# A channel-mixing stage in float32 halves: the third piece's u and gate as seven products of half size, interleaved with the other pieces' products

## The chip, the core and the metric

The kernel runs on one core of one Trainium2 chip. The metric is the time of one launch in microseconds (us), measured on the device; three runs of the kernel before gave 943.95, 944.12 and 947.55 us, so its median is 944.12 us.

## What is computed

Two residual layers over 1024 prompt tokens and 64 sample tokens (8 sequences of 8), width 1024. The first is gated linear attention, which the change leaves alone but for the form of its last result. The second is a chunked token-mixing MLP:

```python
def cmlp_mixer(h, w_in, ln_g, ln_b, w_spatial, b_spatial, w_out):
    u, v, gate = jnp.split(h @ w_in, 3, axis=-1)
    v = layernorm(v, ln_g, ln_b)
    ...
    mixed = jnp.einsum('gts,bnsgd->bntgd', ws, vg) + bs.T[:, :, None]
    z = u * mixed.reshape(bsz, t, CMLP_WIDTH) * jax.nn.silu(gate)
    return z @ w_out, v
```

`h` is the RMS-normalised input of the layer. All operands are float32.

## The kernel before, in words

The 1088 tokens are three pieces: 384, 384 and 320 (two chunks of 128 and the 64 sample rows). Activations lie with features on the partitions and tokens in the free dimension. A float32 operand is split into a rounded part and a rest (float32r, `split` L189, `parts_of` L943), and a product of two of them is three matmuls per 128 features: high by high, high by low, low by high.

The v columns of the MLP are made first, in blocks 16 to 19 (L996 to L1038). While that runs, `token_sums` (L912) loads the layer's input again and forms sums of features and of the first two pieces in `tsum`, for what follows.

Then a loop over m = 0 to 7 (L1106 on; a *step* below) makes 128 columns of u and the same 128 columns of gate, multiplies, and stores z. For pieces 0 and 1, the two column blocks (u, gate), the two halves of the features and the two pieces form a 2 by 2 by 2 product, which is made from seven block products in place of eight, each over 4 times 128 features (`product` L986: 12 matmuls of 128x384). The operands of the weights for it are four sums of quarters of the weight block (s1 to s4, `sums` L961, on POOL) and three plain quarters (1,1), (1,2), (2,2). Piece 2 has an odd width and takes the ordinary way: `u` (L1197, L1198) and `gate` (L1204, L1205) are two accumulations of 24 matmuls of 128x320 each, for which a fourth plain quarter (2,1) is needed.

The weight block of a step is a single buffer, `rawq` (L937, `Quarters` L949): 1 MB in four loads. It is loaded for one step ahead when the last plain quarter has been taken out of it. The split operands are in a ring of eight buffers (`wq`, L944). The PSUM banks used here are two each of `misc` (`pb`, `pe`), `mm` (`p1`, `u`, `gate`) and `o` (`mix`).

The normalised v comes back by DMA into `vm` (L1060, two buffers), is normalised by nine ScalarE instructions (`v_norm` L1069) and mixed over the positions of a chunk on TensorE (`mixed` L1084). A small result `v_out` (L1079) is made of it on POOL.

From L993 to the end of the loop, `in_order` (L48) ties each engine to the order in which the code is written: DVE, ACT, POOL, PE and the DMA queue of SP each run their instructions of this stage in exactly that order. After the loop, `out_proj` (L791) multiplies z by the last weights: piece 0 from an operand that is split during the last step, pieces 1 and 2 from z reloaded by DMA (L1236 on).

## Time and profile before

| | before |
|---|---|
| median of three runs | 944.12 us |
| the profiled execution | 945.69 us, of which the span from first to last instruction is 943.9 us |
| granted TensorE clock, mean | 0.995 |
| TensorE busy (matmul) | 909.9 us, 96% of the span |
| VectorE, ScalarE, GpSimd busy | 624.3, 447.0, 305.6 us |
| v blocks 16 to 19 | about 536 to 637 us |
| the loop over m | 637.0 to 832.5 us |
| output projection | from 832.5 us on |

PE is TensorE's matmul, PEld its weight load, DVE VectorE, ACT ScalarE, POOL GpSimd, SP the engine that issues the DMAs. L12 is line 12 of the kernel before. The busy time of the matmuls overlaps itself, since they are pipelined: what a matmul costs in a stream is the distance from its start to the next one's start. In the profile's shapes "128x384" is 128 partitions by 384 elements.

### The profile page before, as it was taken

Reading aid. Unit: us, or ns where it says so; the run is one execution under the profiler, and the core shown is the slowest. Engines: PE = TensorE matmul, PEld = TensorE weight load, DVE = VectorE, ACT = ScalarE, POOL = GpSimd, SP = SyncE. Lnnn points to the kernel's source line nnn. Section 1 sums busy time; section 2 is a strip of 40 time slices with the busy share of each in tenths; the row PEclk is TensorE's granted clock in tenths of the full one; section 3 lists DMA queues with packets and bytes.
Section 4 is the critical chain, followed back from the end, with each engine's and each line's share of the span. In section 5 each row is a group of like instructions: output and inputs, shape, how many; then the busy total and the mean of one; then the engine's idle time right before and its main releaser. Section 6 shows DMA issues by size and latency. Waiting matters only on the chain.

```text
span 943.9 us, 16451 instructions
## 1 busy us (share of the span) xinstructions
PE 909.9 (96%) x6149; PEld 884.2 (94%) x6149; DVE 624.3 (66%) x1239; ACT 447.0 (47%) x940; POOL 305.6 (32%) x315
## 2 busy tenths in 40 slices
PE   9989999999999999989999999999899999989995
PEld 8979989998999899978999999999899999989994
DVE  7888778677885877688552944455666666773246
ACT  7664544454462555464342733336444444454322
POOL 2023332333322331322143121144655555302123
PEclk9999999999999999999999999999999999999998
DMA  9302113311232112324574143523333333384233
GB/s 296 95 1 82 50 36 87 110 38 36 67 103 60 63 41 84 103 83 126 154 255 141 62 152 121 177 73 100 97 97 97 97 97 97 116 259 123 58 109 129
DMA packets 89644, 98.40 MB, mean 104 GB/s; under 512 B 9927, under 2 KB 82061, under 8 KB 89565
## 3 DMA queue, kind: packets, MB, share of 16 engines
q1 hardware_dynamic: 89564, 97.36, 33.6%
q8 instruction: 48, 0.79, 0.3%
q14 instruction: 32, 0.25, 0.1%
HBM read 70.92 MB, written 26.42 MB: 103 GB/s over the span
## 4 chain that ended last, share of the span: by engine, by line
PE 66%; DVE 15%; ACT 6%; issue 6%; DMA 5%; POOL 2%; SPq 1%; DVEq 0%; ACTq 0%; POOLq 0%
PE fm L132 26%; PE tm L146 15%; PE pb L990 4%; PE p L990 3%; PE pe L990 3%; PE u L990 2%; PE gate L990 2%; PE sc L508 2%; PE tms L162 1%; DVE wq L946 1%; PE pst L579 1%; PE mix L1088 1%; DMA xsum<-x_spill 1%; PE o L618 1%; DVE scT L521 1%
## 5 line engine op out<-in xcount | busy, mean ns | idle before, releaser
L146 PE MATMUL tm<-w,h 128*128 128x256 f32 (+1 forms) x1536 | 192.7, 283 | 1.6 <-ACT vt L1001 1.2
L132 PE MATMUL fm<-h,w 128*128 128x384 f32 (+1 forms) x1056 | 188.7, 333 | 0.1
L146 PEld LDWEIGHTS tm<-w,h 128*128 128x128 f32 x1536 | 185.4, 188 | 3.4 <-ACT vt L1001 1.6
L132 PEld LDWEIGHTS fm<-h,w 128*128 128x128 f32 x1056 | 174.4, 188 | 2.0 <-DVE h L196 0.7
L132 PE MATMUL fm<-og,w 128*128 128x384 f32 (+1 forms) x576 | 102.0, 332 | 0.4 <-DVE og L193 0.4
L132 PEld LDWEIGHTS fm<-og,w 128*128 128x128 f32 x576 | 95.1, 188 | 1.6 <-DVE og L193 0.6
L118 DVE TENSOR_TENSOR w<-wr,w 128x512 fp32r<-128x512 f32 (+1 forms) x96 | 71.3, 758 | 21.4 <-ACT w L117 20.6
L117 ACT ACTIVATE w<-wr 128x512 fp32r<-128x512 f32 (+1 forms) x96 | 58.6, 624 | 26.6 <-DMA wr<-w 14.5
L132 PE MATMUL fm<-zs,w 128*128 128x384 f32 (+1 forms) x384 | 64.0, 326 | 1.4 <-DVE x L838 1.4
L816 POOL TENSOR_TENSOR acc<-acc,sq 128x384 f32<-128x384 f32 (+1 forms) x30 | 30.9, 1034 | 105.6 <-ACT sq L811 105.1
L132 PEld LDWEIGHTS fm<-zs,w 128*128 128x128 f32 x384 | 62.3, 188 | 2.6 <-DVE x L838 2.0
L838 DVE TENSOR_TENSOR x<-fm,res 128x384 f32<-128x384 f32 (+1 forms) x40 | 21.0, 527 | 54.5 <-PE fm L132 54.5
L811 ACT ACTIVATE sq<-x 128x384 f32<-128x384 f32 (+1 forms) x42 | 21.0, 503 | 62.2 <-DVE x L838 59.4
L1008 DVE BATCH_NORM_STATS2 st<-vt 128x6 f32<-128x256 f32 (+1 forms) x36 | 15.2, 421 | 42.4 <-ACT vt L1001 42.2
L463 POOL TENSOR_TENSOR xe<-xe,k 128x384 f32<-128x384 f32 (+2 forms) x24 | 28.5, 1187 | 45.2 <-ACT xe L462 42.0
L649 POOL TENSOR_TENSOR on<-on,g 128x384 f32<-128x384 f32 (+1 forms) x24 | 23.8, 1013 | 57.0 <-DVE on L648 34.6
L439 POOL TENSOR_TENSOR kd<-kd,k 128x384 f32<-128x384 f32 (+1 forms) x12 | 12.0, 1004 | 85.8 <-ACT kd L438 85.8
L990 PE MATMUL pb<-tsum,wq 128*128 128x384 f32 x192 | 37.2, 341 | 2.5 <-DVE wq L946 1.4
L990 PEld LDWEIGHTS pb<-tsum,wq 128*128 128x128 f32 x192 | 33.7, 188 | 3.7 <-DVE wq L946 1.8
L990 PE MATMUL p<-h,wq 128*128 128x384 f32 x192 | 36.4, 337 | 0.0
L990 PE MATMUL pe<-tsum,wq 128*128 128x384 f32 x192 | 36.2, 336 | 0.0
L132 PE MATMUL fm<-tsum,w 128*128 128x384 f32 x192 | 34.3, 338 | 1.6 <-DVE z L1199 1.6
(271 smaller groups left out, 1855.2 us busy)
## 6 DMA issues: line engine op xcount, KB each, us to landing
wr<-w SPq DMA_DIRECT2D x92, 256.0 KB, 3.1
rawq<-w SPq DMA_DIRECT2D x32, 256.0 KB, 3.5
s<-s SPq DMA_DIRECT2D x16, 256.0 KB, 5.9
state_s<-ns SPq DMA_DIRECT2D x32, 128.0 KB, 2.5
v_spill<-vt SPq DMA_DIRECT2D x32, 128.0 KB, 1.8
vm<-v_spill SPq DMA_DIRECT2D x8, 512.0 KB, 4.3
xsum<-x_spill SPq DMA_DIRECT2D x8, 384.0 KB, 3.6
z_spill<-zt SPq DMA_DIRECT2D x16, 192.0 KB, 1.9
```

Source lines behind the costliest of these rows:

```text
L117: A.activation(w[:, 0], raw, AF.Copy)
L118: V.tensor_tensor(w[:, 1], raw, w[:, 0].bitcast(F32), ALU.subtract)
L132: PE.matmul(acc, lhs, rhs, start=(k == 0), stop=(k == 23))
L146: PE.matmul(acc, lhs, rhs, start=(k == 0), stop=(k == 23))
L463: G.tensor_tensor(xe, xe, kt_[:, :nl], ALU.mult)
L508: PE.matmul(bank[:, c, 0:192], xe[:, c * P:(c + 1) * P], xl[:, c * 192:(c + 1) * 192], start=True, stop=True)
L649: G.tensor_tensor(o, o, gate[h][:, j, t0:t0 + n], ALU.mult)
L811: A.activation(sq, raw[p][:, m, :], AF.Square)
L816: (V if gain is not None and p == 2 or m == KT - 1 else G).tensor_tensor(total, acc[p], sq, ALU.add)
L838: V.tensor_tensor(raw[p][:, m, :], pa, r, ALU.add)
L990: PE.matmul(acc, lhs, rhs, start=start and k + i == 0, stop=k + i == 5, skip_group_check=not start)
L1008: V.bn_stats(stats[i][:, blk - 16, :], t)
```

## The change

Piece 2 is also made as a 2 by 2 by 2 product. Its 320 columns are re-ordered into two halves of 160, each of one chunk (128) and half of the sample rows (32), and take the place of the two pieces. Per step this is seven products of 12 matmuls of 128x160 in place of the 48 matmuls of 128x320, with the same seven weight operands as the products of pieces 0 and 1. In the code each of the seven products of 384 columns (`pb`, `pe`, `pa`) is followed by one of 160 (`qb`, `qe`, `qa`; the first two in a pair of banks called `two`).

What goes with it:

- The operands of the new sums (`half_load`, `half_sums`, `half_parts`) are made during blocks 18 and 19 and mostly written over parts of `h1` that have been used up; block 19 is computed in the order 6, 7, 8, 3, 4, 5, 0, 1, 2 so that they are. Only `sum4` is new memory. The column scales `rs[2]` are re-ordered in place.
- The quarter (2,1) is no longer split. `vm` has one buffer instead of two, and `v_norm` of a step runs in that step.
- The copies, adds and multiplications of piece 2 follow those of pieces 0 and 1. The mixed values of all pieces go into one tile `zt`, and the SiLU and the last product are one instruction each for all of them: `zt` and `sg` are 2 by 544.
- From step 1 on, the four sums of the next weight block stand early in the step on POOL, ahead of `v_out`. The load of the block after it is issued at the end of the step, behind four stores of z.
- At the end, piece 1's operand for the output projection takes its last block from `zt` directly.

The step's instructions on PE. In both lists one step starts at the first `pb`; `p_...` is the accumulator `pa`, `q_...` is `qa`, `two` is `qb` or `qe`, `xN` counts matmuls, or, for `mix`, products of two matmuls each. Before, step 1:

```order
L990 MATMUL pb<-tsum_6126,wq 128x384 x12
L990 MATMUL pe<-tsum_6127,wq 128x384 x12
L990 MATMUL pb<-tsum_6125,wq 128x384 x12
L990 MATMUL p_7693<-h_0_5912,wq 128x384 x12
L1088 MATMUL mix<-ws,vm 128x128 x6
L990 MATMUL pb<-h_1_6014,wq 128x384 x12
L990 MATMUL pe<-tsum_6128,wq 128x384 x12
L990 MATMUL p_7693<-h_0_5912,wq 128x384 x12
L1088 MATMUL mix<-ws,vm 128x128 x2
L1091 MATMUL mix<-wss,vm 128x64
L990 MATMUL u<-h_2_6079,wq 128x320 x24
L990 MATMUL gate<-h_2_6079,wq 128x320 x24
```

After, a step up to its fifth pair of products:

```order
L1047 MATMUL pb<-tsum_6142,wq 128x384 x12
L1047 MATMUL two<-h_1_6014,wq 128x160 x12
L1047 MATMUL pe<-tsum_6143,wq 128x384 x12
L1047 MATMUL two<-h_1_6014,wq 128x160 x12
L1047 MATMUL pb<-tsum_6141,wq 128x384 x12
L1047 MATMUL two<-h_2_6079,wq 128x160 x12
L1047 MATMUL p_8157<-h_0_5912,wq 128x384 x12
L1047 MATMUL q_8158<-h_2_6079,wq 128x160 x12
L1158 MATMUL mix<-ws,vm 128x128 x6
L1047 MATMUL pb<-h_1_6014,wq 128x384 x12
L1047 MATMUL two<-h_2_6079,wq 128x160 x12
L1158 MATMUL mix<-ws,vm 128x128 x2
```

The two long groups `u` and `gate` are gone; a group of twelve 128x160 stands behind each of the seven groups of 128x384.

On POOL, one turn from the multiplication of `zt` on. `qsum` and `qs` are the sums s1 to s4 of a weight block, `bc` is `v_out`, `p_...` and `q_...` are u and gate values. Before:

```order
L1162 TENSOR_TENSOR zt<-zt,p_7627 128x384
L958 TENSOR_TENSOR qsum<-rawq 128x512
L958 TENSOR_TENSOR qsum<-qsum,rawq 128x512
L1175 TENSOR_TENSOR sg<-sg,rs_80 128x384
L958 TENSOR_TENSOR qsum<-rawq 128x512
L958 TENSOR_TENSOR qs_7783<-rawq,qsum 128x512
L1064 MEMSET vm 64x128
L1221 TENSOR_TENSOR sg_7854<-sg_7854,rs_81 128x320
L1080 TENSOR_TENSOR bc<-vm,bc 64x128
L1081 TENSOR_TENSOR bc<-bc 64x128
L1152 TENSOR_TENSOR p_7866<-p_7866,p_7867 128x384
```

After, from the last multiplication of `sg` of the step before on:

```order
L1277 TENSOR_TENSOR sg<-sg,rs_80 128x384
L1014 TENSOR_TENSOR qsum<-rawq 128x512
L1014 TENSOR_TENSOR qsum<-qsum,rawq 128x512
L1014 TENSOR_TENSOR qsum<-rawq 128x512
L1014 TENSOR_TENSOR qs_8370<-rawq,qsum 128x512
L1149 TENSOR_TENSOR bc<-vm,bc 64x128
L1150 TENSOR_TENSOR bc<-bc 64x128
L1227 TENSOR_TENSOR p_8333<-p_8333,p_8334 128x384
L1228 TENSOR_TENSOR sg<-sg,p_8334 128x384
L1229 TENSOR_TENSOR q_8335<-q_8335,q_8336 128x160
L1230 TENSOR_TENSOR sg<-sg,q_8336 128x160
L1231 TENSOR_TENSOR sg<-sg,rs_80 128x384
```

The sums moved from behind the multiplication of `zt`, late in a step, to the front of the next one, ahead of `bc` and the five additions and multiplications of that step.

On SP's DMA queue, one step from the stores of z on. Before:

```order
L1186 DMA z_spill<-zt 128x384 x2
L1065 DMA vm<-v_spill 128x8x128
L1066 DMA vm<-v_spill 64x128
L1076 DMA bc<-lnbc 64x256
L940 DMA rawq<-w 128x512 x4
L1223 DMA z_spill<-z_7531 128x320
```

After:

```order
L1286 DMA z_spill<-zt 128x384 x2
L1288 DMA z_spill<-zt 128x2x128
L1288 DMA z_spill<-zt 128x2x32
L996 DMA rawq<-w 128x512 x4
L1145 DMA bc<-lnbc 64x256
L1151 DMA v_out<-bc 64x128
```

The load of the weight block now follows four stores of z.

The core of the diff. Of the loop only the lines after are shown; those before are the listing above, L1100 to L1228.

```diff
+NH = 160
...
     def side_by_side(act, name, into):
         hs = into.tile([P, KT, 2, NS], F32R, tag="hs", name=name)
         for part in range(2):
-            G.tensor_copy(hs[:, :, part, :], act[:, part, :, 256:320].bitcast(F32))
+            for lo, hi, at in ((0, NS, 256),) if into is gc else ((0, 32, P), (32, NS, 160 + P)):
+                G.tensor_copy(hs[:, :, part, lo:hi], act[:, part, :, at:at + hi - lo].bitcast(F32))
...
+    def halves(t, natural):
+
+        if natural:
+            return (t[:, lo:hi].rearrange("p (h t) -> p h t", h=2) for lo, hi in ((0, 256), (256, 320)))
+        t = t.rearrange("p (h t) -> p h t", h=2)
+        return t[:, :, :P], t[:, :, P:]
...
+            gain = ng[:, 1, kt:kt + 1]
+            if p < 2:
+                split(h1[p], kt, raw[:, kt, :], gain)
+                continue
+
+            hi, lo = (halves(h1[p][:, i, kt, :], 0) for i in range(2))
+            for dh, dl, src in zip(hi, lo, halves(raw[:, kt, :], 1)):
+                A.activation(dh, src, AF.Copy, scale=gain)
+                V.scalar_tensor_tensor(dl, src, gain, dh.bitcast(F32), ALU.mult, ALU.subtract)
...
+    sum4 = mp.tile([P, 2, 4, NH], F32R, tag="sum4", name="sum4")
+    even = lambda t, lo: [t[:, i].rearrange("p (k e) t -> p k e t", e=2)[:, :, 0, lo:lo + NH] for i in range(2)]
+    tsum2 = [even(h1[2], NH), even(h1[1], 0), even(h1[1], NH), [sum4[:, 0], sum4[:, 1]]]
+    xh = {}
+
+    def half_load(k):
+
+        if k == 0:
+            x = vp.tile([P, 2, 2, NPMAX], F32, tag="xsum", name="xhalf")
+            for i in range(2):
+                xh[i] = [x[:, i, e, :2 * NH].rearrange("p (h t) -> p h t", h=2) for e in range(2)]
+        elif k > 1:
+            xh[k] = [tmp(("ld", "sq")[k - 2], (3, 2)[k - 2], 2 * NH, "xhalf").rearrange("p (h t) -> p h t", h=2)
+                     for _ in range(2)]
+        for e in range(2):
+            row = a["x1_spill"][:, 2 * k + e, SEQ - 256:]
+            for lo, hi, at in ((0, P, 0), (P, NH, 256)):
+                n = 2 * (hi - lo)
+                SP.dma_start(xh[k][e][:, :, lo:hi], row[:, at:at + n].rearrange("p (h t) -> p h t", h=2))
+
+    def half_sums(k):
+        for e in range(2):
+            A.activation(xh[k][e], xh[k][e], AF.Copy, scale=ng[:, 1, 2 * k + e:2 * k + e + 1])
+        b11, b12, b21, b22 = (xh[k][e][:, h, :] for e in range(2) for h in range(2))
+        G.tensor_tensor(b11, b12, b11, ALU.subtract)
+        G.tensor_tensor(b12, b22, b12, ALU.subtract)
+        G.tensor_tensor(b22, b22, b11, ALU.subtract)
+        G.tensor_tensor(b21, b21, b22, ALU.subtract)
+
+    def half_parts(i):
+
+        hi, lo = tsum2[i]
+        for k in range(4):
+            src = xh[k][i in (1, 3)][:, (0, 1, 1, 0)[i], :]
+            A.activation(hi[:, k], src, AF.Copy)
+            V.tensor_tensor(lo[:, k], src, hi[:, k].bitcast(F32), ALU.subtract)
...
-        for i in range(9):
+        for j, i in enumerate((6, 7, 8, 3, 4, 5, 0, 1, 2) if blk == 19 else range(9)):
             t = vp.tile([P, 256], F32, tag="vt", bufs=4, name="vt")
             if i < 8:
-                A.activation(t, tm_block(ws_[blk], h1[i // 3], (i % 3) * P), AF.Copy)
...
+            if blk == 18 and j in (0, 1):
+                half_load(2 + j)
+            if (blk, j) == (18, 2):
+
+                t = tmp("hn", 2, 2 * NH, "rsh")
+                for dst, src in zip(halves(t, 0), halves(rs[2], 1)):
+                    G.tensor_copy(dst, src)
+                G.tensor_copy(rs[2], t)
+            if (blk, j) == (18, 5):
                 nxt = Quarters(20)
             if blk == 19:
+                if j < 2:
+                    half_load(j)
+                if j in (0, 1):
+                    half_sums(2 + j)
+                if j in (2, 3):
+                    half_sums(j - 2)
+                if j in (4, 5, 6, 7):
+                    half_parts((3, 0, 1, 2)[j - 4])
+                if j in (1, 2, 3):
+                    nxt.sums(("s1", "s2", "s3")[j - 1])
+                if j in (3, 4, 5, 6):
+                    if j == 5:
+                        nxt.sums("s4")
+                    if j == 6:
+                        nxt.plain((1, 1))
+                    else:
+                        nxt.parts(("s1", "s2", "s3")[j - 3])
...
-        t = up.tile([P, 9, P], F32, tag="vm", bufs=2, name="vm")
+        t = up.tile([P, 9, P], F32, tag="vm", name="vm")
...
     zs = [None] * 3
+    N, M = NPMAX, NPMAX + NH
+    tq = [[(t[:, 0, k, :], t[:, 1, k, :]) for k in range(4)] for t in tsum]
+    tq2 = [[(hi[:, k], lo[:, k]) for k in range(4)] for hi, lo in tsum2]
+    b11, b21, b22 = quarter(0, 0), quarter(0, 1), quarter(1, 1)
+    half = lambda e, lo: [(x[..., lo:lo + NH], y[..., lo:lo + NH]) for x, y in quarter(2, e)]
+    c11, c21, c22 = half(0, 0), half(1, 0), half(1, NH)
+    rsh = rs[2].rearrange("p (h t) -> p h t", h=2)
     vm = v_load(0)
+    cur, nxt = nxt, None
     for m in range(KT):
+        w, g, more = cur.w, m // 2, m + 1 < KT
+        first = m == 0
+        bias = up.tile([P, P], F32, tag="bias", name="bias")
+        zt = up.tile([P, 2, M], F32, tag="zt", name="zt")
+        sg = up.tile([P, 2, M], F32, tag="sg", name="sg")
         bc = v_out_load(m)
         pb, pe = ps("misc", "pb")[:, :N], ps("misc", "pe")[:, :N]
+        two = pp.tile([P, 2, 512], F32, tag="sc4", name="two")
+        qb, qe = two[:, 0, :NH], two[:, 1, :NH]
         p6, p1 = tmp("sq", 2, N, "p6"), tmp("sq", 2, N, "p1")
+        q6, q1 = tmp("hn", 2, NH, "q6"), tmp("hn", 2, NH, "q1")
         product(pb, w["s2"], tq[1])
+        product(qb, w["s2"], tq2[1])
+        A.activation(p6, pb, AF.Copy)
         V.scalar_tensor_tensor(bias, rsum[:, g, :], lnb[:, m:m + 1], bs[:, g, :], ALU.mult, ALU.add)
+        if first:
+            cur.parts("s4")
+        A.activation(q6, qb, AF.Copy)
+        if first:
+            cur.plain((2, 2))
+        elif more:
+            for key in ("s1", "s2", "s3", "s4"):
+                nxt.sums(key, up if key == "s4" else None)
+        product(pe, w["s3"], tq[2])
+        product(qe, w["s3"], tq2[2])
+        A.activation(sg[:, 1, :N], pe, AF.Copy)
+        if first:
+            cur.plain((1, 2))
+            nxt = Quarters(21)
+        A.activation(sg[:, 1, N:], qe, AF.Copy)
+        v_norm(vm)
+        v_out(m, vm, bc)
+        product(pb, w["s1"], tq[0], start=False)
+        product(qb, w["s1"], tq2[0], start=False)
+        V.tensor_tensor(sg[:, 1, :N], sg[:, 1, :N], pb, ALU.add)
+        V.tensor_tensor(sg[:, 1, N:], sg[:, 1, N:], qb, ALU.add)
+        if more and not first:
+            nxt.parts("s2")
+        pa, qa = ps("mm", "p1")[:, :N], ps("mm", "q1")[:, :NH]
+        product(pa, w[1, 1], b11)
+        product(qa, w[1, 1], c11)
+        A.activation(p1, pa, AF.Copy)
+        A.activation(q1, qa, AF.Copy)
+        G.tensor_tensor(p6, p6, p1, ALU.add)
+        G.tensor_tensor(sg[:, 1, :N], sg[:, 1, :N], p1, ALU.add)
+        G.tensor_tensor(q6, q6, q1, ALU.add)
+        G.tensor_tensor(sg[:, 1, N:], sg[:, 1, N:], q1, ALU.add)
+        G.tensor_tensor(sg[:, 1, :N], sg[:, 1, :N], rs[1], ALU.mult)
+        for p in range(2):
+            mixed(zt, vm, g, m, bias, p)
+        if more and not first:
+            nxt.parts("s3")
+            nxt.parts("s1")
+        if not more:
+
+            zs[0] = Halves(tsum[1], tsum[2])
+            for kt in range(3):
+                split(zs[0], kt, stage[:, kt, :])
+        product(pb, w["s4"], b22, start=False)
+        product(qb, w["s4"], c22, start=False)
+        V.tensor_tensor(p1, p1, pb, ALU.add)
+        V.tensor_tensor(q1, q1, qb, ALU.add)
+        G.tensor_tensor(zt[:, 1, :N], zt[:, 1, :N], p1, ALU.mult)
+        mixed(zt, vm, g, m, bias, 2)
+        G.tensor_tensor(zt[:, 1, N:], zt[:, 1, N:], q1, ALU.mult)
+        if more:
+            vm = v_load(m + 1)
+            if first:
+                for key in ("s1", "s2", "s3", "s4"):
+                    nxt.sums(key, up if key == "s4" else None)
+            else:
+                nxt.plain((1, 1))
+                nxt.parts("s4")
         else:
             for kt in range(3, 7):
+                split(zs[0], kt, stage[:, kt, :] if kt < 5 else rest[kt - 5])
             load_w(28, 1)
             load_w(28, 2)
         product(pe, w[2, 2], tq[3], start=False)
+        product(qe, w[2, 2], tq2[3], start=False)
+        V.tensor_tensor(sg[:, 0, :N], p6, pe, ALU.add)
+        V.tensor_tensor(sg[:, 0, N:], q6, qe, ALU.add)
+        V.tensor_tensor(sg[:, 0, :N], sg[:, 0, :N], rs[0], ALU.mult)
+        V.tensor_tensor(sg[:, :, N:], sg[:, :, N:], rsh, ALU.mult)
         A.activation(sg, sg, AF.Silu)
+        if first:
+            for key in ("s2", "s3", "s1"):
+                nxt.parts(key)
+        elif more:
+            nxt.plain((2, 2))
+        else:
+            fetch_w(28, [0, 1])
+            load_w(28, 3)
+        G.tensor_tensor(sg[:, 1, :N], sg[:, 1, :N], rs[1], ALU.mult)
         product(pa, w[1, 2], b21, start=False)
+        product(qa, w[1, 2], c21, start=False)
+        V.tensor_tensor(sg[:, 0, :N], sg[:, 0, :N], rs[0], ALU.mult)
+        V.tensor_tensor(sg[:, :, N:], sg[:, :, N:], rsh, ALU.mult)
+        V.tensor_tensor(zt[:, 0, :N], pa, zt[:, 0, :N], ALU.mult)
+        V.tensor_tensor(zt[:, 0, N:], qa, zt[:, 0, N:], ALU.mult)
         V.tensor_tensor(zt, zt, sg, ALU.mult)
         for p in range(2):
+            SP.dma_start(z_d[:, m, p * N:p * N + N], zt[:, p, :N])
+        for lo, hi, at in ((N, N + P, 2 * N), (N + P, M, SEQ)):
+            SP.dma_start(z_d[:, m, at:at + 2 * (hi - lo)].rearrange("p (h t) -> p h t", h=2), zt[:, :, lo:hi])
         if more:
+            if first:
+                nxt.plain((1, 1))
+                nxt.parts("s4")
+                nxt.plain((2, 2))
+            nxt.plain((1, 2))
+            if m + 2 < KT:
+                following = Quarters(22 + m)
+            else:
+                stage = mp.tile([P, 5, N], F32, tag="rawq", name="zstage")
+                SP.dma_start(stage, z_d[:, 0:5, 0:N])
+                rest = [wp.tile([P, N], F32, tag="raw", bufs=3, name="zmore") for _ in range(2)]
+                for i, t in enumerate(rest):
+                    SP.dma_start(t, z_d[:, 5 + i, 0:N])
+                load_w(28, 0)
+                following = None
+            cur, nxt = nxt, following
         else:
+            for p in range(2):
+                if p:
+                    zs[p] = act_slot(p, f"zs{p}")
+                split(zs[p], 7, zt[:, p, :N])
+            fetch_w(28, [2, 3])
```

More of the change, by code (lines that the diff above doesn't have):

```diff
@@ L1082, in v_out, with mixed @@
         SP.dma_start(a["v_out"][:, m * P:(m + 1) * P], bc[:, 2, :])
[L1084 removed]
+    def mixed(dst, vm, g, m, bias, p):
         pm = ps("o", "mix")
+        nch = PIECES[p][2]
         for c in range(nch):
[L1088 to L1098 removed]
@@ L1100, in trunk_kernel @@
-    zs = [None] * 3
+            PE.matmul(pm[:, c * P:(c + 1) * P], vm[:, 3 * p + c, :], ws[:, g, :], start=True, stop=True)
+        gain = lng[:, m:m + 1]
+        if p < 2:
+            V.scalar_tensor_tensor(dst[:, p, :N].rearrange("p (c t) -> p c t", c=nch),
+                                   pm[:, :N].rearrange("p (c t) -> p c t", c=nch), gain, over(bias, nch),
+                                   ALU.mult, ALU.add)
+            return
+        PE.matmul(pm[:, 256:256 + NS], vm[:, 8, :], wss[:, g, :], start=True, stop=True)
@@ L1148, in trunk_kernel @@
-        if more:
-            v_norm(vnext, range(9) if m == 0 else range(6, 9))
-        if m == 0:
-            v_out(m, vm, bc)
-        G.tensor_tensor(p6, p6, p1, ALU.add)
-        G.tensor_tensor(sg[:, 1, :], sg[:, 1, :], p1, ALU.add)
-        G.tensor_tensor(sg[:, 1, :], sg[:, 1, :], rs[1], ALU.mult)
-        for p in range(2):
-            mixed(zt[:, p, :], vm, g, m, bias, 3 * p, 3, False)
-        if not more:
-            for kt in range(3):
-                split(zs[0], kt, nxt[:, kt, :])
@@ L1187, in trunk_kernel @@
         if more:
-            nxt.sums("s3")
-            nxt.sums("s4", up)
-            for key in ("s2", "s1", "s3"):
-                nxt.parts(key)
-        else:
-            split(zs[0], 7, zt[:, 0, :])
-            fetch_w(28, [1, 2, 3])
-        u = ps("mm", "u")[:, :size[2]]
-        product(u, w[1, 1], quarter(2, 0))
-        product(u, w[1, 2], quarter(2, 1), start=False)
-        V.tensor_tensor(z2, u, z2, ALU.mult)
-        if more:
-            nxt.parts("s4")
-            nxt.plain((1, 1), (1, 2))
```

152 lines of the change are left out of this document (28 added, 124 removed).

## The prediction

> **What bounds the kernel now.** I read the busy time by stretches first, then the chain of waits through the loop over m, then who makes PE wait there. In the middle of the loop (columns: stretch, its length, busy us and instructions of PE, PEld, DVE, ACT and POOL, granted clock, DMA share, GB/s):
>
> ```profile
> 688.00:800.00 112.00, 112.00 (x705) 112.00 (x704) 70.89 (x108) 49.35 (x104) 64.51 (x62) 1.00 0.32 95
> ```
>
> PE has no gap at all in these 112 us, at full clock, while DVE is busy for 63% and POOL for 58%. The chain of waits (start, length, what) says the same: for one whole step it is PE alone.
>
> ```profile
> 697.97 2.09 PE pb L990 x12
> 700.06 2.12 PE pe L990 x12
> 702.18 2.11 PE p L990 x12
> 704.29 0.44 PE mix L1088 x4
> 704.74 0.17 PE mix L1091 x2
> 704.91 3.58 PE u L990 x24
> 708.48 3.52 PE gate L990 x24
> 712.00 2.11 PE pb L990 x12
> 714.11 2.08 PE pe L990 x12
> ...
> 720.42 1.34 PE mix L1088 x12
> 721.76 0.35 PE pb L990 x2
> ```
>
> From 697.97 to 721.76 is one step: 23.79 us. Of it `u` and `gate` take 7.09 us (704.91 to 712.00), 148 ns for each of 48 matmuls; a product of 384 columns takes 2.1 us. The loop's first and last matmul groups, and the two other places where PE waits in it:
>
> ```profile
> 637.01 2.66 PE L990 MATMUL pb<-tsum,wq 128*128 128x384 f32 x12
> ...
> 832.52 8.67 PE L132 MATMUL fm<-tsum,w 128*128 128x384 f32 x48 [1.58 <-DVE z L1199]
> ...
> PE pb L990 <- DVE wq L946: 1.4, 1, 1.4
> PE pb L990 <- ACT p L1125: 1.1, 1, 1.1
> ```
>
> From 637.01 to 832.52 the loop lasts 195.5 us, 5.2 us more than eight steps, and 4.1 us of that are the three waits shown.
>
> **Part 1, the matmuls.** The change takes 48 matmuls of 320 columns out of a step and puts in 84 of 160: 15,360 columns become 13,440. If time went by columns this would save 0.9 us per step. So the question is what a matmul costs whose columns are few, with new weights for each. The trace shows it in the attention stage (start, length, engine; an `x8` is eight in a row):
>
> ```profile
> 138.10 0.40 PE L146 MATMUL tm<-w,h 128*128 128x256 f32 x2
> 138.60 0.19 PEld L529 LDWEIGHTS sc<-x1h,ones_r 128*128 128x128 f32 x1
> 138.75 0.24 PE L529 MATMUL sc<-x1h,ones_r 128*128 128x160 f32 x1
> 138.75 0.30 PEld L146 LDWEIGHTS tm<-w,h 128*128 128x128 f32 x2
> 138.82 0.43 PE L146 MATMUL tm<-w,h 128*128 128x256 f32 x2
> 155.21 1.03 PEld L618 LDWEIGHTS o<-qd,s 128*128 128x128 f32 x8
> ```
>
> The one matmul of 160 columns, in the same number format as the change's, is followed by the next after 0.07 us. That looks cheap, but its successor pays: the two matmuls of 256 then take 0.43 us, where two of them alone take 0.40. So the narrow one cost 0.10 us. The reason is in the PEld rows: a load lasts 0.19 us, two of them 0.30, so loads start 0.11 us apart. Eight loads for matmuls of only eight columns take 1.03, which is 0.12 apart. A load of 128 columns of weights thus occupies the loader for 0.11 us, and only one load is ahead of the matmul that runs. Under 384 or 320 columns (175 and 148 ns) it is hidden; under 160 it is not. It does not help that high by high and high by low use the same weights: in the attention rows the weights were the same tile of ones, and were loaded again.
>
> I take 0.111 us per narrow matmul, with 0.10 and 0.12 as ends. A step's narrow products then cost 84 x 0.111 = 9.3 us, against 7.1: the step goes from 23.79 to 26.0 us on PE, +2.23, over eight steps +17.8 us (ends: +10.5 and +24).
>
> The Trainium skill, TensorE: Matmul & The Clock Gate, section Back-to-back issue gap, gives N / 2.4 + 2.5 ns between isolated matmuls; that is 69 ns for 160 columns (an estimate from that page), 5.8 us per step, a gain. By this rule the change pays on PE; the rows above speak against it. The same page's section on LDWEIGHTS gives the columns divided by 1.2, 107 ns for 128 (an estimate from it), with which the measured 0.11 agrees.
>
> **Part 2, the way of the weights.** PE is not alone any more: one weight block of 1 MB is staged at a time, and the change puts its load and its sums into one closed circle with the step's own arithmetic. Its steps, with their rows (for DVE, ACT, POOL groups: busy us, mean ns; for single lines: shortest, median, longest ns):
>
> ```profile
> L1186 SPq DMA_DIRECT2D z_spill<-zt x16: 325/359/423, 661.4 to 829.4; - x16
> 649.90 1.78 SPq L940 DMA_DIRECT2D rawq<-w  x4
> 655.71 1.29 POOL L958 TENSOR_TENSOR qsum<-rawq 128x512 f32<-128x512 f32 x1 [3.28 <-DMA rawq<-w]
> L958 POOL TENSOR_TENSOR qsum<-rawq 128x512 f32<-128x512 f32 x14 | 20.0, 1432 | 3.3 <-DMA rawq<-w 3.3
> L958 POOL TENSOR_TENSOR qs<-rawq,qsum 128x512 f32<-128x512 f32 x7 | 14.0, 2006 | 0.0
> L958 POOL TENSOR_TENSOR qsum<-qsum,rawq 128x512 f32<-128x512 f32 x7 | 10.2, 1461 | 0.6
> L1153 POOL TENSOR_TENSOR sg<-sg,p 128x384 f32<-128x384 f32 x8 | 8.1, 1012 | 0.0
> L1080 POOL TENSOR_TENSOR bc<-vm,bc 64x128 f32<-64x128 f32 x8 | 6.5, 809 | 6.5 <-ACT vm L1072 6.2 <-DMA bc<-lnbc 0.2
> L1081 POOL TENSOR_TENSOR bc<-bc 64x128 f32<-64x128 f32 x8 | 4.6, 571 | 0.6
> L946 DVE TENSOR_TENSOR wq<-rawq,wq x32: 671/678/2626, 640.4 to 809.8; 128x512 fp32r<-128x512 f32 x32
> L1092 DVE SCALAR_TENSOR_TENSOR z<-mix,lng,bias 128x256 f32<-128x256 f32 x8 | 3.8, 472 | 0.0
> L1161 DVE TENSOR_TENSOR p<-p,pb 128x384 f32<-128x384 f32 x8 | 4.4, 551 | 9.4 <-PE pb L990 9.4
> L1170 DVE TENSOR_TENSOR sg<-sg,rs 128x384 f32<-128x384 f32 x8 | 5.5, 683 | 0.3
> L1184 DVE TENSOR_TENSOR zt<-zt,sg x8: 941/1460/2036, 659.4 to 828.0; 128x768 f32<-128x768 f32 x8
> L1171 ACT ACTIVATE sg<-sg 128x768 f32<-128x768 f32 x8 | 6.8, 846 | 37.3 <-DVE sg L1170 37.3
> ...
> L1171 ACT ACT_TABLE_LOAD x1 | 1.3, 1283 | 2.3 <-DVE sg L1170 2.3
> ```
>
> Start behind the last product of a step, `zt` by `sg`. SP issues four stores of z before the load: 4 x 0.36 = 1.4. From the first of four `rawq` loads to POOL's first sum 649.90 to 655.71 = 5.8, POOL being idle. The four sums, 2 x 1.43 + 1.46 + 2.01 = 6.3. `v_out` stands behind them: 0.81 + 0.57 = 1.4. Then the additions of `p1`, two of 1.01 and two of 160 columns at about 0.5: 3.0. Only then may DVE write over `p1` and `q1`; q1's addition 0.3, the mixed values of piece 2 0.47 + 2 x 0.25, two weight parts 1.4, the sums with `pe` and `qe` 0.55 + 0.3, the scalings 0.68 + 0.5: together 4.7. SiLU of 1088 columns, 0.85 x 1088/768 = 1.2. A weight part through ACT and DVE, twice 0.68: 1.4. Two more scalings and the products with `pa` and `qa`: 0.68 + 0.5 + 0.55 + 0.3 = 2.0. Last `zt` by `sg` with 1088 columns, between 1.3 (from the shortest) and 2.9 (from the longest); POOL is idle then, so 1.5. The figures for 160 columns are estimates by width from the rows of 384. The circle: 1.4 + 5.8 + 6.3 + 1.4 + 3.0 + 4.7 + 1.2 + 1.4 + 2.0 + 1.5 = 28.7 us, ends 27.3 (if the stores' 1.4 cost nothing) and 30.9 (`zt` by `sg` at 2.9, two parts at 1.1 each, between their median and longest).
>
> One turn is one step, so a step can't be shorter than 28.7 on average, against 26.0 on PE. Before, the load left early in the step and landed long before its sums, which stood late on POOL: no circle. It does not bind at once. In the settled state a step's first `pb` waits for DVE's addition to `p1` of the step before, since both use one bank; from there to the end of `zt` by `sg` I count, from the terms above, 0.4 + 0.3 + 1.0 + 1.4 + 0.85 + 1.2 + 1.2 + 1.4 + 2.0 + 1.5 = 11.2 us, and 0.7 for the last part, after which the next load may leave: 11.9 us into a step. In step 0 `qe` ends at 22.6 us (26.0 less the last pair of products, 2.1 + 1.3). Sums and scalings 2.0, SiLU with its table 1.3 + 1.2: 27.1. The first part for step 1, through ACT and DVE, follows it, so step 1 starts at 28.0 instead of 26.0. Two more parts 1.4, scalings and products 2.0, `zt` by `sg` 1.5, four parts 2.8 end at 35.7, which is 7.7 us into step 1. The lead of 11.9 - 7.7 = 4.2 is used up at 2.7 per step after a step and a half: step 2 takes about 1 us more than 26.0, and steps 3 to 6 take 28.7.
>
> **Part 3, the ends.** Of before's waits the two of 1.4 and 1.1 go; step 0 waits 2.0, as worked out. Step 7 needs z of steps 0 to 4 in `rawq`:
>
> ```profile
> 810.74 5.37 DMA zstage<-z_spill
> ```
>
> It leaves behind the four stores 11.2 + 1.4 = 12.6 us into step 7 and lands at 18.0. On DVE there follow, at the prices above and about 0.5 for a split of 384 columns: three splits 2.0 with ACT's first half, the additions to `p1` and `q1` 0.85, mixed 1.0, four splits 2.0, sums 0.85, scalings 1.2; SiLU 1.2; two output weights 2.1; scalings 1.2, and the product that frees `pa`'s bank 0.55: 31.0 us into the step the output projection's first matmul starts. It then waits some 2 for its last two weight quarters, which follow the splits of z on ACT and DVE. Before, `u` and `gate` lay over this. What is added in blocks 16 to 19 (16 loads, about 50 short instructions) I cost at nothing: ACT, DVE and POOL have half their time free there; ends -1 and +2.
>
> **The sum.** Step 0 is 28.0, steps 1 and 2 53.0, steps 3 to 6 at 28.7 114.8, step 7 31.0, its last weights 2.0: 228.8 us, against 195.5, so +33.3. The profiled execution took 945.69 us (span 943.9), 1.6 above the median of the runs; 944.12 + 33.3 gives 977.4 us.
>
> **The rivals.** *The loader alone.* If the circle closes in under 26.0 us (DMA faster, operations overlapped that I put in a row), PE sets the step: 8 x 26.0, 2.0 in step 0 and 3 to 5 us in step 7 as before and after it: 213 to 215, +17.5 to +19.5, about 963. For it: the circle's sum has estimates in it, and would have to shrink by only 10%. Against it: my sum counts no hand-over between engines.
>
> *Faster.* Narrow matmuls stream at the 0.07 us that separates the starts, the weights being ahead. Then 84 x 0.075 = 6.3 us, a step of 23.0, and with the waits gone -5 to -8 us: about 938. It decides below 7.09 / 84 = 84 ns per narrow matmul. By the Trainium skill's gap rule, cited in part 1, it would go this way. Against it stand the pair's 0.43 and the eight loads in 1.03; it needs the circle under 23 us as well.
>
> *No change*: the narrow matmuls near 84 ns with a circle under 24. Nothing in the trace gives that price.
>
> *Much slower*: the circle at 30.9 us because DVE and POOL hinder each other (a part of 0.68 us once took 2.6). The lead then lasts less than one step, so steps 3 to 6 take 2.2 more each than in the sum, and step 2 another 4: +46, about 990.
>
> **How the numbers follow.** Circle and loader, 966 to 988: 0.68, with 977.4 the likeliest. Loader alone, 958 to 966: 0.20. Above 988: 0.06. Faster 0.04, no change 0.02. The range 958 to 988 leaves out little more than a tenth; both its ends come from the ends of the two prices. A measurement of this kernel can tell about 0.5%, 4.7 us, from no change; slower by more than that: 0.94.
>
> **What would show it.** In the profile after, matmuls of 128x160 in a row start 0.11 us apart (0.075 would refute part 1). The starts of `pb` are 26 us apart at first and 28 to 29 from step 3 on (26 throughout would refute part 2, and leave the loader). POOL's first sum waits for the DMA of `rawq`, DVE's addition to `p1` waits for POOL, and PE's first `pb` of a step waits for that. The output projection's first matmul waits several us for DVE. The prediction is wrong if steps are under 24 us, or if most of the time goes to blocks 16 to 19.

## The result, and the profile after

| | before | after |
|---|---|---|
| median of the runs | 944.39 us (943.95 to 947.55, 4 runs) | 989.1 us (986.46 to 989.53, 4 runs) |
| profiled execution, its span | 945.69, 943.9 us | 988.94, 987.2 us |
| loop over m: first `pb` to first matmul of the output projection | 195.5 us | 237.9 us |
| ratio of the runs | | 1.046 (95%: 1.0431 to 1.0489) |

The change makes the kernel 44.7 us slower, where 33.3 was forecast. Its 989.1 us lie 1.1 above the upper end of the forecast's range, 988; by the ratio of the runs, 1.046 x 944.12 = 987.5, they lie just inside it. The spans of the two profiled executions differ by 43.3 us, and the 42.4 by which the loop is longer are nearly all of it: the part ahead of the loop takes 0.5 us more (its first matmul starts at 637.50 in place of 637.01), and the part behind it 0.3.

PE's groups at the loop's first and last matmul (start, length; in brackets how long PE stood idle ahead and what ended it):

```profile
637.50 2.65 PE L1047 MATMUL pb<-tsum,wq 128*128 128x384 f32 x12
...
875.43 4.77 PE L134 MATMUL fm<-tsum,w 128*128 128x384 f32 x17 [2.73 <-DVE zt L1282]
```

The stretch that had no gap before (length, then busy us of PE, PEld, DVE, ACT, POOL, then granted clock, DMA share, GB/s):

```profile
688.00:800.00 112.00, 104.26 (x709) 102.73 (x708) 56.45 (x99) 39.34 (x85) 48.92 (x56) 0.97 0.26 82
```

PE now stands idle for 7.7 of 112 us, at a granted clock of 0.97, and DVE and POOL are less busy than before (56 us against 71, 49 against 65). An engine that is overloaded does not look like that; a chain of waits does. In the chain, `x12` is one product; first three products at the loop's start, then one turn between two first sums of POOL:

```profile
640.15 1.30 PE two L1047 x12
641.45 2.15 PE pe L1047 x12
643.60 1.30 PE two L1047 x12
```

```profile
709.90 1.27 POOL qsum L1014
711.26 1.35 POOL qsum L1014 x2
712.61 1.15 issue
713.76 1.72 POOL qs L1014
715.48 0.88 POOL bc L1149
716.42 0.79 POOL bc L1150
717.21 0.97 POOL p L1227
718.18 0.95 POOL sg L1228
...
721.15 2.50 DVE wq L1002 x2
...
726.32 0.62 ACT wq L1001
726.97 1.15 DVE wq L1002
...
729.79 1.30 DVE zt L1284
731.11 0.34 SPq L1286
731.54 0.39 SPq L1286
732.02 0.40 SPq L1288
732.47 0.49 SPq L1288
733.05 0.44 SPq L996
...
734.49 4.17 DMA rawq<-w
738.82 1.28 POOL qsum L1014
```

The first block is the loader: a narrow product takes 1.30 us, 0.108 per matmul, beside 2.15 for one of 384 columns. The second is the circle, closed: from 709.90 to 738.82 the chain passes through POOL, DVE, ACT, SP and a DMA and never through PE. PE only follows. Who waits longest (us in total, times, longest):

```profile
POOL qsum L1014 <- DMA rawq<-w: 72.3, 6, 13.0
...
DVE p L1244 <- POOL sg L1228: 13.6, 6, 2.3
...
PE two L1047 <- DVE q L1245: 10.1, 6, 2.5
```

POOL stands 72 us for the raw quarters, in six turns; before, 3.3 us. DVE's addition to `p1` waits for POOL, as forecast. PE waits too, but not where the forecast put it: not at a step's first `pb`, but at `qe`, the last but one of the narrow products of the step before.

### The profile page after: what moved, and what is told of

It is laid out like the page before. It is cut to its first block, busy times and chain, and to the rows that moved or that the text cites. A ratio compares the mean times of both kernels' runs of the same rounds, so it can differ in the third digit from the quotient of the medians.

```text
span 987.2 us, 17220 instructions
## 1 busy us (share of the span) xinstructions
PE 940.3 (95%) x6437; PEld 912.7 (92%) x6437; DVE 620.9 (63%) x1287; ACT 457.1 (46%) x980; POOL 313.6 (32%) x352
## 4 chain that ended last, share of the span: by engine, by line
PE 54%; DVE 19%; POOL 6%; issue 6%; DMA 6%; ACT 5%; SPq 2%; DVEq 0%; POOLq 0%; ACTq 0%
PE fm L134 24%; PE tm L148 17%; DMA rawq<-w 3%; DVE wq L1002 2%; POOL qsum L1014 2%; PE two L1047 1%; PE pb L1047 1%; PE sc L511 1%; POOL qs L1014 1%; DVE scT L524 1%; PE o L621 1%; PE pst L582 1%; PE tms L165 1%; DVE w L120 1%; DMA wr<-w 1%
## 5 line engine op out<-in xcount | busy, mean ns | idle before, releaser
L134 PE MATMUL fm<-og,w 128*128 128x384 f32 (+1 forms) x576 | 104.2, 337 | 0.4 <-DVE og L196 0.4
L134 PEld LDWEIGHTS fm<-og,w 128*128 128x128 f32 x576 | 97.2, 192 | 1.6 <-DVE og L196 0.6
L120 DVE TENSOR_TENSOR w<-wr,w 128x512 fp32r<-128x512 f32 (+1 forms) x96 | 70.2, 746 | 26.4 <-ACT w L119 25.4
L1047 PEld LDWEIGHTS two<-h,wq 128*128 128x128 f32 x384 | 47.5, 192 | 0.0
L1047 PE MATMUL two<-h,wq 128*128 128x160 f32 x384 | 46.9, 272 | 0.0
L1002 DVE TENSOR_TENSOR wq<-qsum,wq 128x512 fp32r<-128x512 f32 x25 | 21.3, 875 | 36.8 <-ACT wq L1001 36.8
L1014 POOL TENSOR_TENSOR qsum<-rawq 128x512 f32<-128x512 f32 x16 | 20.8, 1303 | 72.4 <-DMA rawq<-w 72.3
L1047 PE MATMUL pb<-tsum,wq 128*128 128x384 f32 x192 | 39.2, 353 | 3.0 <-ACT wq L1001 2.5
L1047 PE MATMUL p<-h,wq 128*128 128x384 f32 x192 | 41.1, 368 | 0.0
L442 POOL TENSOR_TENSOR kd<-kd,k 128x384 f32<-128x384 f32 (+1 forms) x12 | 11.9, 993 | 85.8 <-ACT kd L441 85.8
```

What stands on the lines that cost most here:

```text
L120: V.tensor_tensor(w[:, 1], raw, w[:, 0].bitcast(F32), ALU.subtract)
L134: PE.matmul(acc, lhs, rhs, start=(k == 0), stop=(k == 23))
L1002: V.tensor_tensor(w[:, 1], src, w[:, 0].bitcast(F32), ALU.subtract)
L1014: G.tensor_tensor(t, x, y, op)
L1047: PE.matmul(acc, lhs, rhs, start=start and k + i == 0, stop=k + i == 5, skip_group_check=not start)
```

## The experiments

Each ratio below is to the kernel before on the same chip: its median was 944.39 us beside the first run of the changed kernel, 947.55 beside e1 to e4, 947.47 beside e6 to e9, 946.95 beside the last three. Loop, turn and half clock are of the profiled execution, in us: the turn is the mean distance of POOL's first sums from step 1 to step 6, the half clock the time in the loop at a granted clock of 0.5.

| kernel | us | ratio (95%) | loop | turn | half clock |
|---|---|---|---|---|---|
| after | 989.1 | 1.046 (1.0431 to 1.0489) | 237.9 | 29.5 | 17.1 |
| after, once more | 989.56 | 1.0445 (1.0391 to 1.0498) | 237.0 | 29.6 | 14.7 |
| e1, before with narrow matmuls | 978.03 | 1.0311 (1.028 to 1.0342) | 227.2 | | 3.4 |
| e2, stores behind the load | 984.62 | 1.0378 (1.0346 to 1.041) | 230.3 | 28.2 | 6.8 |
| e3, two tiles | 988.4 | 1.0425 (1.0399 to 1.0452) | 236.7 | 29.6 | 20.2 |
| e4, load earlier | 972.03 | 1.0245 (1.0214 to 1.0277) | 219.6 | (25.7) | 6.8 |
| e6, narrow products cut | 984.67 | 1.0393 (1.037 to 1.0415) | 231.9 | 30.0 | 56.6 |
| e7, e8 with them cut | 957.83 | 1.0111 (1.0084 to 1.0138) | 204.6 | 24.4 | 34.4 |
| e8, e4 and the first part early | 972.65 | 1.0265 (1.0243 to 1.0288) | 218.3 | (25.5) | 3.4 |
| e9, e8 with equal halves | 962.7 | 1.0154 (1.0131 to 1.0176) | 208.8 | 24.4 | 10.2 |
| e10, e8 and step 0's load early | 969.4 | 1.0235 (1.0194 to 1.0277) | 215.5 | (25.4) | none |
| e11, e10 with equal halves, `v_out` late | 950.9 | 1.0048 (1.0026 to 1.007) | 198.4 | 23.6 | 1.9 |

In brackets: there PE holds the steps at 26.14 us, and POOL's sums follow it (from one step to the next they come a little earlier in the step, so that their distance is below 26.14).

**e1: the loader by itself.** The kernel before, its `u` and `gate` in halves of 160 columns.

```
+        cut = lambda e, lo: [(x[..., lo:lo + 160], y[..., lo:lo + 160]) for x, y in quarter(2, e)]
-        product(u, w[1, 1], quarter(2, 0))
-        product(u, w[1, 2], quarter(2, 1), start=False)
+        for lo in (0, 160):
+            product(u[:, lo:lo + 160], w[1, 1], cut(0, lo))
+            product(u[:, lo:lo + 160], w[1, 2], cut(1, lo), start=False)
```

(and `gate` alike).

> The kernel before, with its third piece's u and gate each made as two halves of 160 columns: 96 matmuls of 160 columns a step in place of 48 of 320, the same columns in sum, the same operands. Loader theory (a matmul starts no sooner than one 128-column weight load, 0.111 us, after the last): 96 x 0.111 = 10.7 us in place of 48 x 0.147 = 7.1, so +3.6 us a step, +28 us over eight steps: 970 to 975 us. Column theory (a matmul costs its columns at 0.45 ns and a few ns more): 0 to +2 us: 944 to 947 us.

978.03 us, ratio 1.0311: +30.5 us where +28 was expected. The chain over one step of e1, where it is PE alone:

```profile
712.35 5.38 PE u L990 x48
717.72 5.36 PE gate L990 x48
```

10.74 us for 96 matmuls is 0.112 each, in place of 7.10 for the same columns in 48; the steps are 27.44 us in place of 23.79, +3.65. The column theory is refuted: with no other edit, halving the columns and doubling the count costs 3%. Eight steps of +3.65 make 29.2 of the 31.7 us by which e1's loop is longer. The rest is PE's wait at the loop's end, 7.1 us in place of 1.6, less the two waits of the first steps, which are gone (e1's half clock falls into the wait at the end):

```profile
867.41 2.90 PE L132 MATMUL fm<-tsum,w 128*128 128x384 f32 x8 [7.12 <-DVE z L1201]
```

**e2, e4: shortening the circle.** e2 issues the four z stores behind the next raw load in steps 1 to 5 (`z_store` holds the four):

```
...
+        if first or m + 2 >= KT:
+            z_store()
...
                 following = Quarters(22 + m)
+                if not first:
+                    z_store()
```

e4 moves, in steps 1 to 5, the last split and the load up behind SiLU:

```
         elif more:
             nxt.plain((2, 2))
+            if m + 2 < KT:
+                nxt.plain((1, 2))
+                following = Quarters(22 + m)
```

> The changed kernel, with the four z stores of steps 1 to 5 issued on SyncE behind the load of the next raw quarters rather than ahead of it. Circle theory (a turn through the one buffer of raw quarters sets the step): the 1.4 to 2.9 us between zt's last product and the load's first part leave the turn in five steps: -8 to -13 us, 976 to 981 us. Loader alone (TensorE's own work sets the step): no change, 986 to 990 us.

> The changed kernel, with the splitting of the last quarter and the load of the next raw quarters moved ahead of the scalings, zt's products and the z stores in steps 1 to 5. Circle theory: the turn loses the scalings and products (1.7 to 2.0 us), zt by sg (1.3 to 1.5) and the stores (1.4 to 2.9), and becomes 24 to 25 us, below the 26.0 us that TensorE's loads and matmuls need, so that steps 3 to 6 fall from 29.9 to 26.0 to 26.5: about -20 us, 966 to 972 us, with the clock at full speed through the loop. What is left over the kernel before is the loader's +18. Rival (what sets the steps is DVE's or ScalarE's own work, which stays): -5 us at most.

e2: 1.0378, 6 to 8 us less than the changed kernel in its two measurements, short of the 8 to 13 expected. Its interval lies below that of the first measurement and overlaps that of the second; the traces say the same as the times, with a loop 7 us shorter than in either and a turn that falls by 1.3 us, from 29.5 to 28.2. e4: 1.0245, 19 to 20 us less. A change of order alone, with not one instruction fewer, gives back nearly half of the loss. The stretch of e4's steps 3 to 6:

```profile
724.00:828.00 104.00, 104.00 (x742) 104.00 (x741) 62.80 (x104) 42.89 (x94) 54.40 (x61) 1.00 0.28 88
```

PE has no gap and full clock, and a step is 26.14 us: the loader's price, forecast as 26.0.

**e3: the wait that I thought false.** `qb` and `qe` are two banks of one tile, and PE's program in the changed kernel waits at `qe` for DVE to have read `qb`. e3 gives them a tile each.

```
...
-        two = pp.tile([P, 2, 512], F32, tag="sc4", name="two")
-        qb, qe = two[:, 0, :NH], two[:, 1, :NH]
+        qb, qe = (qp.tile([P, 512], F32, tag=t, name=t)[:, :NH] for t in ("qb", "qe"))
```

> The changed kernel, with the two sums of the sample rows in two tiles of one bank each in place of the two banks of one tile. Theory of the false wait (the third product of a step waits for DVE's reading of the other bank because both are one tile, which takes the lead of the first steps): TensorE runs on to the next reuse of a bank 4.8 us later, the lead of about 4 us is back in steps 1 and 2, and then the circle of 29.5 us holds it as before: -4 to -6 us, 983 to 985 us, and less time at half clock. Rival (the wait is of the circle, wherever it falls): no change within 1 us, 987 to 990 us. Rival (the half clock after the waits is what makes the steps long): -10 us or more.

988.4 us, 1.0425: not to be told from the changed kernel (1.0445 and 1.046). The loop is 1.2 us shorter. PE's waits in e3's loop:

```profile
PE mix L1160 <- ACT wq L1002: 10.0, 5, 3.2
PE fm L134 <- DVE zt L1283: 5.5, 1, 5.5
```

The wait at `qe` is gone (at 747.57 `qe` now starts ahead of DVE's reading of `qb`, at 748.29), and the same 10 us stand two groups earlier in PE's order, at the third `mixed` group, that of piece 2, whose bank DVE reads behind the first weight part; that part waits for ACT, ACT for POOL's sums, the sums for `rawq`. The theory fell in what it promised. The two banks did share a wait, but the time was the circle's, and taking away the place where it showed moved it.

**e6, e7: is PE in the circle?** Both keep three of each narrow product's twelve matmuls, so the third piece's `u` and `gate` are sums over a quarter of their rows.

```
-        for k in range(4):
+        for k in range(4 if acc.shape[-1] > NH else 1):
...
```

> The changed kernel, with each narrow product (u and gate of the third piece) cut from twelve matmuls to its first three: 63 matmuls of 160 columns a step fall out, 7.0 us of TensorE's time, and the third piece's u and gate are sums over a quarter of their rows; all else stays. Circle theory (the turn of 29.5 us holds the steps and TensorE's narrow matmuls aren't in it): the steps stay at 29 to 30 us, less 1 us at most where a product lies between two of the turn's steps: 975 to 989 us. Loader theory (the narrow matmuls' 0.111 us each set the steps): -56 us, about 933 us.

> The kernel of e8 with the narrow products cut to their first three matmuls as in e6 (the third piece's u and gate are sums over a quarter of their rows). It shows the length of the turn once the load is moved ahead, with TensorE out of the way (19 us of work a step). By the terms of the turn: 5.8 load + 5.5 sums + 1.7 v_out + 2.9 additions + 5.1 to the scalings + 1.1 SiLU + 2.0 two splits = 24.1 us a step: some -10 us against e8. If no circle through the buffer exists: -50 us.

e6 takes 7 us of work a step from PE, 56 us in all, and the time falls by 5 to 6 us; the turn stays at 30.0. POOL's first sums:

```profile
703.85 1.26 POOL L1014 TENSOR_TENSOR qsum<-rawq 128x512 f32<-128x512 f32 x1 [12.53 <-DMA rawq<-w]
734.77 1.26 POOL L1014 TENSOR_TENSOR qsum<-rawq 128x512 f32<-128x512 f32 x1 [13.29 <-DMA rawq<-w]
764.40 1.26 POOL L1014 TENSOR_TENSOR qsum<-rawq 128x512 f32<-128x512 f32 x1 [12.00 <-DMA rawq<-w]
```

A part of what e6 saves goes to half clock, but PE still stands idle for 55 us of the loop, against 18 in the changed kernel. There PE's speed hardly matters to the loop. e7 asks the same of the shortened circle, and its sums stand 24.4 us apart, where the terms of the turn had given 24.1:

```profile
699.41 1.29 POOL L1014 TENSOR_TENSOR qsum<-rawq 128x512 f32<-128x512 f32 x1 [6.16 <-DMA rawq<-w]
723.70 1.29 POOL L1014 TENSOR_TENSOR qsum<-rawq 128x512 f32<-128x512 f32 x1 [6.60 <-DMA rawq<-w]
747.86 1.29 POOL L1014 TENSOR_TENSOR qsum<-rawq 128x512 f32<-128x512 f32 x1 [6.46 <-DMA rawq<-w]
```

The time fell by 14.8 us against e8, where 10 was expected; step 0, which is not held by the turn, is 6.3 us shorter too (20.1 in place of 26.5). So the sum of terms is good to about 1%, and at 24.4 the circle lies under PE's 26.1, which is why e4 reaches the loader's price and no less.

**e8, e10: the first steps.** In e4 PE still waited 2.5 us between steps 0 and 1, and step 1 took 29.45 us. e8 puts the split of `s2` for step 1 ahead of the last scaling before SiLU in step 0; e10 also puts step 0's last four splits and its load ahead of the scalings that follow SiLU (the lines from `nxt.plain((1, 1))` on, which stood at the step's end).

```
+        if first:
+            nxt.parts("s2")
         V.tensor_tensor(sg[:, :, N:], sg[:, :, N:], rsh, ALU.mult)
         A.activation(sg, sg, AF.Silu)
         if first:
-            for key in ("s2", "s3", "s1"):
+            for key in ("s3", "s1"):
                 nxt.parts(key)
+            nxt.plain((1, 1))
+            nxt.parts("s4")
+            nxt.plain((2, 2), (1, 2))
+            following = Quarters(22)
```

> The kernel with the load moved ahead (the run e4), and in step 0 alone the split of the first sum of step 1's quarters moved ahead of the scaling before SiLU, so that TensorE no longer waits 2.5 us for it between the steps 0 and 1. If a wait of that length is what brings the half clock (0.5 for some microseconds at the start of step 1, which there takes 29.45 us in place of 26.14), both go: -5 to -6 us against that kernel, 1.019 times the kernel before. If the half clock has another cause: -2.5 us alone, and step 1 stays near 29 us.

> The kernel of e8, with step 0's last four splits and its load of raw quarters also moved ahead of the scalings, zt's products and the z stores. In e8 TensorE waited 3.2 us in step 1, on the chain from that load (issued at 677.2 us, 10 us after step 0's SiLU), and lost 1.7 us more to half clock. Circle theory: the load leaves some 4 us earlier, the waits and the half clock go, all eight steps are the 26.1 us of TensorE's loads and matmuls: -4 to -5 us against e8, 1.021 to 1.023 times the kernel before; what is left is the loader's +17.8 us and the end. Rival (step 0's own products come so much later that step 1 waits for sg's one buffer): no change against e8.

e8 missed: 1.0265, no change against e4, where both of its theories had expected a gain. Step 0 became 26.48 in place of 29.16 us, and step 1 31.45 in place of 29.45:

```profile
688.23 0.68 PE L1158 MATMUL mix<-ws,vm 128*128 128x128 f32 x4 [1.68 <-ACT wq L1001]
...
688.89 3.77 PE L1047 MATMUL pe<-tsum,wq 128*128 128x384 f32 x12
693.71 1.57 PE L1047 MATMUL two<-sum,wq 128*128 128x160 f32 x12 [1.05 <-DVE q L1245]
```

PE came 2.7 us earlier to a place that the load of step 0 held, waited there, and ran the next product at half clock (3.77 us in place of 2.15). Moving that load (e10) takes 2.8 us more off the loop, and steps 2 to 6 are 26.14 each, with no gap on PE and no half clock:

```profile
694.00:850.00 156.00, 156.00 (x1111) 156.00 (x1110) 96.66 (x158) 64.38 (x141) 76.04 (x85) 1.00 0.30 94
```

Step 1 still takes 28.65, where 26.1 was expected. The gain against e8 is 0.3%, inside the intervals, where 0.4 to 0.5% was expected. e10's loop is 20.0 us longer than that of the kernel before, and 8 x (26.14 - 23.79) = 18.8 of it are the loader.

**e9, e11: what the columns would cost if split evenly.** A probe of the time alone: each product's 544 columns as 272 and 272 in place of 384 and 160, all read from columns of the first two pieces; the third piece's own columns are left out. e11 also moves `v_out` on POOL behind `zt`'s products.

```
+    E = M // 2
+    cols = lambda t: [(x[..., :E], y[..., :E]) for x, y in t]
...
-        product(pb, w["s2"], tq[1])
-        product(qb, w["s2"], tq2[1])
+        product(pb, w["s2"], cols(tq[1]))
+        product(qb, w["s2"], cols(tq[1]))
...
+            v_out(m, vm, bc)
             vm = v_load(m + 1)
```

> The kernel of e8 with the 544 columns of each product split into 272 and 272 in place of 384 and 160, as many matmuls as before (168 a step). It is a probe of the time alone: the products read columns of the first two pieces, so that u and gate are wrong. Loader theory: the 128x272 matmuls of the first stage follow each other by 0.125 us, above the 0.111 of a weight load, so nothing is lost to the loader: 168 x 0.125 + 2.0 = 23.0 us of TensorE a step in place of 26.0; the turn of about 24.1 us then holds the steps: -10 us against e8, about 1.008 times the kernel before. Column theory (a matmul costs its columns and a fixed part each, whatever the split): the sum of columns and the count are the same, no change against e8.

> The kernel of e10 with the columns split 272 and 272 as in e9 (a probe of the time alone: u and gate are wrong, being made of columns of the first two pieces) and with v_out's two operations moved on POOL from ahead of the additions to behind zt's products. The turn loses v_out's 1.7 us: 24.4 - 1.7 = 22.7 us, just below TensorE's 23.1 (measured for a step of e9 without a wait). Steps of 23.1 to 23.5 us, in place of the 23.8 of the kernel before: loop 189 to 192 us against 195.5: 0.995 to 1.0 times the kernel before. Rival (the turn keeps its 24.4 us because its additions wait for TensorE or ScalarE rather than for v_out): 1.01.

e9: 1.0154, 10 us under e8 as forecast (the 1.008 was reckoned from a faster e8 than came), with the same number of matmuls and of columns, so the price is neither the count nor the columns. PE's chain in e9 at a place without a wait:

```profile
698.15 1.51 PE pb L1047 x12
699.66 1.51 PE two L1047 x12
701.16 1.50 PE pe L1047 x12
```

1.51 us for twelve is 0.126 each, above the 0.111 of a load; a step without a wait is 23.15 us. The circle's 24.4 holds the others. e11 takes `v_out` out of it: a circle of 22.7 was expected, below PE's own 23.15, and so steps of 23.1 to 23.5; the turns are 23.6. The ratio of 1.0048 lies between the 0.995 to 1.0 forecast and the rival's 1.01. Step 1 is still 28.8 us, with waits of 0.3 to 1.3 us each for ACT and DVE, and PE waits 4.1 us at the loop's end. No version here beats the kernel before.

## Why the prediction was right in its cause and short by 9 us in the loop

**The loader: right.** The forecast was 0.111 us per narrow matmul and a step of 26.0; the runs give 0.108 to 0.112 and 26.14. The rival that narrow matmuls stream at 0.07 us is refuted by e1 alone. A fixed time per matmul of 0.11 us, whatever it loads, would fit e1 and e9 as well; the trace of the kernel before speaks against it. In its attention stage six loads of only 64 columns of weights, one of which lasts 0.14 us, go by in 0.42, so they start 0.06 us apart, and so do their matmuls of 64 columns:

```profile
143.51 0.42 PEld L499 LDWEIGHTS sc<-x 128*64 128x64 f32 x6
143.51 0.56 PE L499 MATMUL sc<-x 128*64 128x64 f32 x6
```

The loads of 128 columns in the forecast's rows, for matmuls of only eight columns, start 0.12 apart: the price goes with the weights.

The Trainium skill, TensorE: Matmul & The Clock Gate, has both rules: its N / 2.4 + 2.5 ns (section Back-to-back issue gap) gives 69 ns for 160 columns and 116 for 272 (estimates from that page). The section gives it for an isolated matmul and says itself that it counts too little at small N, where it has no share for the load. With a load for each matmul the runs show 108 to 112 and 126, so it is low in both, and misleads at 160, where the load of the Trainium skill's section LDWEIGHTS on the same page (107 ns, an estimate from it) is the longer of the two.

**The circle: right in kind, 3% short in size.** The turn was forecast at 28.7 us and is 29.5. In the turn shown (28.9 us) the terms are, measured against forecast: sums 5.6 (6.3), `v_out` 1.7 (1.4), additions 2.9 (3.0), to the scalings 5.2 (4.7), SiLU 1.0 (1.2), a part 1.8 (1.4), scalings and products 1.7 (2.0), `zt` by `sg` 1.3 (1.5), stores 1.9 (1.4), load 5.8 (5.8). Two kinds of term came out longer. The stores take 1.9 us here, 2.9 in the turn before, where they leave from 701.47 and the load at 704.36, and 2.3 on average of the five turns; e2 confirms that this term is in the turn (-1.3 us each). The weight parts are the other: the two within "to the scalings" take 2.50 us where 1.4 was counted, and the part behind SiLU 1.8 in place of 1.4. That the sums and some short operations came out shorter hid most of it. The parts' DVE operations are long where one of POOL's runs beside them:

```profile
721.01 0.99 POOL L1246 TENSOR_TENSOR zt<-zt,p 128x384 f32<-128x384 f32 x1
721.07 1.98 DVE L1002 TENSOR_TENSOR wq<-rawq,wq 128x512 fp32r<-128x512 f32 x1
721.97 0.53 POOL L1248 TENSOR_TENSOR zt<-zt,q 128x160 f32<-128x160 f32 x1
722.97 0.68 DVE L1002 TENSOR_TENSOR wq<-qs,wq 128x512 fp32r<-128x512 f32 x1
```

In the loop the 20 with no POOL operation beside them take 0.68 to 0.69 us, the other 32 take 0.71 to 1.99. That POOL's operation is the cause is read from these durations; no run here separates it.

**The lead: wrong.** The forecast's step was: "In the settled state a step's first `pb` waits for DVE's addition to `p1` of the step before", so that the load leaves 11.9 us into a step, 7.7 at first, and 4.2 us of lead last for a step and a half. No first `pb` from step 2 on waits at all. PE is held 4.7 to 7.5 us of its work earlier, at `qe` and at the third `mixed` group. The loads leave 6 to 9 us into a step from the first one on (the first at 7.7, as forecast; 704.36 is 8.7 us into step 2, which starts at 695.65; 733.05 is 6.2 into step 3, from 726.89), so there was no lead to use up. Steps 0 to 7 by their first `pb`: 29.1, 29.0, 31.2, 27.4, 31.7, 28.0, 32.5, 29.0 us, where 28.0, 53.0 for two, 28.7 four times and 33.0 were forecast. What this cost shows at the end. As in the forecast, time into the loop is counted from its first matmul. Step 6's `zt` by `sg` ends 211.5 us into the loop, where 207.0 was forecast: +4.5, from step 0 (+1.1) and five turns of 0.8 more, less small terms. From there to the output projection's first matmul it takes 26.5 us in place of 21.8, +4.7, because PE comes into step 7 only 2.6 us ahead of that product (11.2 forecast), and its 19 us up to the third `mixed` group lie on the path. Together that is 9.1 (4.47 + 4.66), and 33.3 + 9.1 = 42.4.

**The split of the 42.4 us.** The loader is 18.8. Order alone, with no instruction less (e4, e8, e10), takes the loop from 237.9 to 215.5: 22.4 us for the circle and the waits that it causes. 1.2 us are left for the waits of the first steps and the end.

**The rivals.** The loader alone, forecast as 213 to 215 us for the loop, is what e10 is (215.5). "Much slower", 990 us, met the time without its circle of 30.9 us: the turn is 29.5. The hindrance between DVE and POOL that it named shows in the weight parts, as above, but not in `zt` by `sg`, which it put at up to 2.9 us and which took 1.29 in all eight steps:

```profile
L1284 DVE TENSOR_TENSOR zt<-zt,sg x8: 1285/1291/1294, 670.6 to 876.5; 128x1088 f32<-128x1088 f32 x8
```

What stands in place of its longer turns is the way from step 6 to the output projection, +4.7 us, which it did not name.

**Left open.** A second buffer of raw quarters would break the circle outright, at 8 KB more per partition; it wasn't tried. Why e11's turn is 0.5 us over PE's 23.15 was not separated.

## What to carry to other kernels

Count what a smaller matmul leaves to the weight loader before counting columns: where the columns stream in less time than one load takes (0.111 us here for 128 columns of weights; 160 columns were below it, 272 above), splitting work into fewer multiplications with more loads loses. When a change makes one buffer's load, its use and the arithmetic behind it depend on each other in a ring, add up the ring and compare it with the busiest engine; if it is longer, look for steps of the ring that need not be in it, as the stores and the last products here. A wait that disappears without a gain was only the place where a longer chain showed: follow the chain to the buffer that closes it.
